# A fused two-block transformer kernel: new durations in the planner that orders its instructions

## The chip, the cores and the metric

One core of one Trainium2 chip runs the whole program. The metric is the device time of one execution in microseconds (us), the median of several runs; lower is better.

## What is computed

The input is 512 tokens of width 1024, all in fp32. The first block normalises x, projects it, runs three branches, merges them through sigmoid gates, and ends with a wide feed-forward layer. The second block has two layers, each of attention (eight softmax heads with a forget gate, eight retention heads), a gated convolutional feed-forward layer, and a gated addition. Cut to what matters here:

```python
h = rmsnorm(x, norm_mix_g)
a_q, a_k, a_v, b_q, b_f, b_i, b_g, c_q, c_kv, c_kr, gate_logits = split(h @ w_in)
y_a = chunked_relpos_attention(a_q, a_k, a_v, rel_bias)
y_b = hgrn2_recurrence(b_q, b_f, b_i, b_g, lower_bound, hgrn_norm_g)
y_c = mla_attention(c_q, c_kv, c_kr, positions, ...)
merged = sum(sigmoid(gate_logits[n]) * (y_n @ w_branch[n]) for n in branches)
x = x + merged @ w_out
x = x + square(relu(rmsnorm(x) @ w_ff1)) @ w_ff2
x = rmsnorm(x, final_norm_g)
for i in range(2):
    x = x + concat(forgetting_attention(...), retention(...)) @ w_out_2[i]
    x = x + (gelu(conv(up_a)) * up_g) @ w_down[i]
    x = x + sigmoid(rmsnorm(x) @ w_ple_gate[i]) * (p[i] @ w_ple_proj[i])
return rmsnorm(x, final_norm_w)
```

## The kernel before, in words

Activations lie feature-major: a tile of 128 features by 512 tokens. A projection (`proj`, `multi`, `group`; tiles `lin`) makes one block of 128 outputs. To keep fp32 precision, weights and activations are split into a high and a low half (`wh`, `wl`, `xh`, `xl`), and each 128-row step takes three passes on TensorE: `wh` with `xh`, `wl` with `xh`, `wh` with `xl` (`lin`, matmul line L379). A chunk of weights arrives by DMA as `raw`; ScalarE makes `wh` from it, VectorE makes `wl` (128x1024), and a finished block is taken out of PSUM by VectorE (`gate<-lin`, `qk<-lin`). The token-major values (`v`) are built in the same way.

Attention works by head: scores in `sc`, softmax on VectorE, ScalarE and GpSimd, transposes in `pt` (L389), the product with the values in `po`. The second branch (HGRN, functions `hgrn`, `hlev`, `level`, `dsplit`, `rsplit`) takes four pairs of heads. For each pair it walks nine levels of distance s = 1, 2, 4 ... 256. Per level ScalarE makes two exponentials (`eq`, `ek`), VectorE multiplies `eq` and updates two running sums (`suf`, `pre`), GpSimd multiplies `ek`, TensorE multiplies the two (`sc<-eq,ek`, with 64 contraction rows), and VectorE keeps the result (`dg`). After the last level VectorE makes the low halves (`sl`), TensorE takes the product with the values (`po<-sh,vs` and `po<-sl,vs`), and a per-head norm follows: ScalarE `tl`, VectorE `y`, ScalarE `sq`, TensorE transposes `gs`, VectorE `rs` and `ms`, GpSimd `rt` and `ex`, TensorE transposes `pb`, VectorE `qk`, ScalarE `xh`, VectorE `xl`. That `xh` and `xl` is the branch's output of the pair, `yb[pair]`. The merge of the branch (`up`) takes all four pairs: its first block can run nine passes on the first three pairs and then needs the fourth.

The order of the work is made while the program is built. Each piece of work is a coroutine (a Python generator); it writes out instructions and yields where the next one would have to wait. The projections form one long list of tasks (`stream`) at the lowest priority, and the driver (`drive`) takes them whenever no other coroutine is ready. "Ready" is judged by a clock kept in the program: `self.now` moves on by a number for each matmul (`mm`, `tr`), and for VectorE, ScalarE and GpSimd the class `Eng` adds up an estimated duration for each instruction (`net.busy`). A coroutine that waits for VectorE is taken up again when `self.now` has passed that engine's estimated end plus 200 ns (`w`, `LAT`). So these numbers choose how many passes of projections are put between two steps of a branch. Once built, every engine runs its own list strictly in the order written; semaphores alone hold it back. In the program all VectorE, ScalarE and GpSimd instructions are recorded through one line, L221.

## Time and profile before

| what | value |
|---|---|
| median of 3 runs | 2363.28 us (2362.02 to 2363.62) |
| profiled execution, span from first to last instruction | 2362.3 us |
| what lies around the span in the profiled execution | not shown; the median of the runs is 1.0 us above the span |
| TensorE busy | 2326.2 us, 98% of the span |
| VectorE busy | 1509.7 us, 64% |
| ScalarE busy | 1070.2 us, 45% |
| GpSimd busy | 455.0 us, 19% |
| mean granted TensorE clock | 0.994 |
| chain that ended last | 91% TensorE, 6% VectorE |

How to read it: TensorE is busy nearly the whole time, so the time is the passes plus the moments in which TensorE waits. Shares over the whole span say little about a stretch, and the stretch decides here: from 307 to 508 us the HGRN branch runs, with projections between its levels. The ends of matmuls are modelled, and the steps from start to start tell more than their durations.

### The profile page before, as it was taken

To read this page: it belongs to the slowest core of one execution; us is meant where nothing else is said; L and a number is where in the kernel's file an instruction comes from. 1 tells how busy PE (TensorE), PEld (TensorE's weight loads), DVE (VectorE), ACT (ScalarE), POOL (GpSimd) and SP (SyncE) were. 2 spreads that over 40 slices of the span, in tenths; PEclk is the share of its full clock that TensorE was granted. 3 is DMA by queue.
4 is the path that set the end of the run, shared out by engine and by line. 5 is a ranking of instruction groups with operands and counts; after the bars stand their busy time and mean duration, and the time that the engine had idled before them with its cause. 6 is when DMAs were issued, how large, how long until landed. Compare 5 with 4: busy or idle time off the path is not lost.

```text
span 2362.3 us, 28970 instructions
## 1 busy us (share of the span) xinstructions
PE 2326.2 (98%) x10810; PEld 1871.6 (79%) x10810; DVE 1509.7 (64%) x2355; ACT 1070.2 (45%) x1695; POOL 455.0 (19%) x531
## 2 busy tenths in 40 slices
PE   9999999999999999999999999999999999999998
PEld 7787877778888888777778888888777778888887
DVE  6778489976542554678866562457578866552466
ACT  5657466664321233555543331245555544331343
POOL 3423044431000002323330000002323320000012
PEclk9999999999999999999999999999999999999999
DMA  5222222223322332432332333333332332333332
GB/s 181 75 68 63 81 72 63 63 85 116 98 95 98 98 98 83 152 95 89 117 98 94 98 98 98 104 93 115 123 104 81 107 107 90 98 98 98 107 91 70
DMA packets 75725, 228.23 MB, mean 97 GB/s; under 512 B 9664, under 2 KB 15680, under 8 KB 75584
## 3 DMA queue, kind: packets, MB, share of 16 engines
q1 hardware_dynamic: 70400, 209.62, 28.2%
q0 software_dynamic: 5184, 16.75, 2.3%
q8 instruction: 85, 1.39, 0.3%
q14 instruction: 56, 0.46, 0.1%
HBM read 215.29 MB, written 6.32 MB: 94 GB/s over the span
## 4 chain that ended last, share of the span: by engine, by line
PE 91%; DVE 6%; issue 1%; ACT 1%; POOL 1%; DMA 0%; SPq 0%; POOLq 0%; DVEq 0%; ACTq 0%
PE lin L379 75%; PE v L379 6%; PE sc L379 5%; PE po L379 3%; PE pt L389 1%; DVE wl L221 1%; DVE dg L221 1%; DVE xl L221 1%; DVE eq L221 1%; DVE pre L221 0%; DVE suf L221 0%; DVE sl L221 0%; DVE gate L221 0%; ACT L221 0%; PE pb L389 0%
## 5 line engine op out<-in xcount | busy, mean ns | idle before, releaser
L379 PE MATMUL lin<-xh,wh 128*128 128x512 f32 (+1 forms) x2752 | 1095.9, 398 | 0.0
L379 PE MATMUL lin<-xl,wh 128*128 128x512 f32 (+1 forms) x2752 | 1072.4, 390 | 6.7 <-DVE xl L221 6.6
L379 PE MATMUL lin<-xh,wl 128*128 128x512 f32 (+1 forms) x2728 | 1061.8, 389 | 0.0
L221 DVE TENSOR_TENSOR wl<-raw,wh 128x1024 fp32r<-128x1024 f32 (+3 forms) x391 | 467.6, 1196 | 513.4 <-PE lin L379 335.7
L221 ACT ACTIVATE wh<-raw 128x1024 fp32r<-128x1024 f32 (+4 forms) x394 | 392.5, 996 | 821.7 <-PE lin L379 684.9
L379 PEld LDWEIGHTS lin<-xl,wh 128*128 128x128 f32 x2752 | 517.3, 188 | 117.7 <-DVE xl L221 8.8
L379 PEld LDWEIGHTS lin<-xh,wh 128*128 128x128 f32 x2752 | 517.4, 188 | 117.0 <-issue 11.7
L379 PEld LDWEIGHTS lin<-xh,wl 128*128 128x128 f32 x2728 | 514.2, 188 | 96.1
L221 POOL TENSOR_TENSOR sq<-sq 128x512 f32<-128x512 f32 (+1 forms) x61 | 90.6, 1485 | 571.5 <-ACT sq L221 570.8
L221 POOL TENSOR_SCALAR P<-P,r 128x128 f32<-128x128 f32 (+3 forms) x128 | 80.3, 633 | 198.7 <-DVE r L221 180.8
L221 POOL MEMSET pad<- 128x2 f32 x44 | 4.4, 100 | 586.7 <-DVE cv L221 586.7
L221 DVE SCALAR_TENSOR_TENSOR cv<-pad,vec,cv 128x512 f32<-128x512 f32 x88 | 66.1, 752 | 40.7 <-ACT cv L221 39.0
L221 DVE CUSTOM_DVE_ANT_0 lg<-sc,E 128x128 f32<-128x128 f32 (+1 forms) x96 | 46.6, 486 | 60.9 <-PE sc L379 53.7
L379 PE MATMUL v<-wh,xh 128*128 128x512 f32 x192 | 78.2, 407 | 2.3 <-POOL wh L221 2.3
L379 PE MATMUL v<-wl,xh 128*128 128x512 f32 x192 | 75.6, 394 | 1.5 <-DVE wl L221 1.4
L221 ACT ACTIVATE ph<-pt 128x512 fp32r<-128x512 f32 (+3 forms) x128 | 55.7, 435 | 45.5 <-PE pt L389 44.5
L379 PE MATMUL v<-wh,xl 128*128 128x512 f32 x192 | 75.5, 393 | 0.0
L221 ACT ACTIVATE P<-lg,m 128x128 f32<-128x128 f32 (+1 forms) x96 | 53.5, 558 | 39.7 <-DVE m L221 28.9
L221 DVE TENSOR_TENSOR x<-lin,x 128x512 f32<-128x512 f32 x80 | 54.6, 684 | 23.5 <-PE lin L379 23.4
L221 DVE TENSOR_TENSOR pl<-pt,ph 128x512 fp32r<-128x512 f32 (+3 forms) x128 | 60.4, 481 | 13.8 <-ACT ph L221 13.3
L221 ACT ACT_TABLE_LOAD x51 | 65.4, 1283 | 4.3 <-DVE qk L221 1.6
L221 ACT ACTIVATE tl<-po 64x512 f32<-64x512 f32 x56 | 33.2, 593 | 74.0 <-PE po L379 73.6
(243 smaller groups left out, 2558.6 us busy)
## 6 DMA issues: line engine op xcount, KB each, us to landing
raw<-wup SPq DMA_DIRECT2D x88, 512.0 KB, 3.3
raw<-w SPq DMA_DIRECT2D x83, 512.0 KB, 3.6
raw<-wf SPq DMA_DIRECT2D x64, 512.0 KB, 3.3
raw<-wdn SPq DMA_DIRECT2D x32, 512.0 KB, 3.5
raw<-wv SPq DMA_DIRECT2D x22, 512.0 KB, 3.6
raw<-wpg SPq DMA_DIRECT2D x16, 512.0 KB, 3.3
raw<-wbr SPq DMA_DIRECT2D x12, 512.0 KB, 3.3
raw<-wdn SPq DMA_DIRECT2D x16, 384.0 KB, 3.1
```

The source lines that it names most:

```text
L221: r = f(*a, **k)
L379: self.nc.tensor.matmul(out, l, r, start=start, stop=stop)
L389: self.nc.tensor.transpose(out, src, self.ident)
```

## The change

It replaces the numbers of the program's clock; nothing that is computed changes. A pass with 512 columns counts 226.8 ns where it counted 215.8; a switch between matmuls of 128 and of 64 contraction rows now counts 110 or 185 ns; VectorE counts 155 + 1.05 n ns where it counted 75 + 1.042 n + 60 per scalar operand; ScalarE 140 + 0.84 n + 60 per operand in place of 100 + 0.84 n + 93. GpSimd's numbers stay. Comments and docstrings are taken out too, which shifts line numbers (the matmul is L380, the transpose L394).

```diff
             if name == "dv":
-                d = 75.0 + 1.042 * n + 60.0 * ops
+                d = 155.0 + 1.05 * n
             elif name == "ac":
-                d = 100.0 + 0.84 * n + 93.0 * (ops + ("accum_out" in k))
+                d = 140.0 + 0.84 * n + 60.0 * (ops + ("accum_out" in k))
...
     def mm(self, out, l, r, start, stop):
         self.nc.tensor.matmul(out, l, r, start=start, stop=stop)
         n = int(np.prod(out.shape[1:]))
+        rows = 64 if l.shape[0] <= 64 else 128
+        if rows != self.rows:
+            self.now += 110.0 if rows == 64 else 185.0
+            self.rows = rows
         if l.dtype == F32:
-            self.now += 112.0 if n == 64 else max(218.0, n * 4 / 2.4 + 5)
+            self.now += 112.0 if n == 64 else 152.0 if rows == 64 else max(218.0, n * 4 / 2.4 + 27)
         elif l.dtype == BF16:
             self.now += n / 2.4 + 2.5
         else:
-            self.now += max(107.0, n / 2.4 + 2.5)
+            self.now += max(109.0, n / 2.4 + 13.5)
 
     def tr(self, out, src):
         self.nc.tensor.transpose(out, src, self.ident)
-        self.now += 112.0
+        self.rows = 128
+        self.now += 109.0
```

The change moves instructions on all engines, by the thousand, since every later choice follows from an earlier one. Two places matter most; both lie at the end of the HGRN branch, at its fourth pair.

TensorE, last product with the values of the fourth pair, before:

```order
L379 MATMUL po<-sh,vs 128x128
L379 MATMUL po<-sl,vs 128x128
L379 MATMUL lin<-xh,wh 128x512
L379 MATMUL lin<-xh,wl 128x512
L379 MATMUL lin<-xl,wh 128x512
```

and now:

```order
L380 MATMUL po<-sh,vs 128x128
L380 MATMUL po<-sl,vs 128x128
L394 MATMUL gs<-cst,sq 128x128 x4
L394 MATMUL pb<-cst,ex 128x128 x4
L380 MATMUL lin<-xh,wh 128x512
L380 MATMUL lin<-xh,wl 128x512
L380 MATMUL lin<-xl,wh 128x512
```

Before, 21 projection passes stand between the product and the transposes `gs`, and 27 more between `gs` and `pb`. Now none stand there; `pb` follows `gs` at once, and the next passes are those that need the fourth pair's output.

VectorE, the norm of the same pair, before:

```order
L221 TENSOR_TENSOR y<-po,tl 64x512 x2
L221 TENSOR_TENSOR wl<-raw,wh 128x1024
L221 TENSOR_TENSOR gate<-lin,rb 128x512
L221 TENSOR_REDUCE rs<-gs 128x8
L221 TENSOR_SCALAR ms<-rs 128x8
```

and now:

```order
L221 TENSOR_TENSOR y<-po,tl 64x512 x2
L221 TENSOR_REDUCE rs<-gs 128x8
L221 TENSOR_SCALAR ms<-rs 128x8
L221 SCALAR_TENSOR_TENSOR qk<-y,vec,qk 128x512
L221 TENSOR_TENSOR qk<-pb,qk 128x512
L221 TENSOR_TENSOR xl<-qk,xh 128x512
```

The weight halves (`wl`) and the gates' blocks (`gate<-lin`) that stood between the steps of the norm are done earlier now, among the levels of the pairs.

## Rows read from the trace of the kernel before

**Rows 1.** The page, part 1: the span, and TensorE's busy time.

```profile
span 2362.3 us, 28970 instructions
PE 2326.2 (98%) x10810; PEld 1871.6 (79%) x10810; DVE 1509.7 (64%) x2355; ACT 1070.2 (45%) x1695; POOL 455.0 (19%) x531
```

**Rows 2.** Waits of TensorE: line waited for what, us in total, times, longest.

```profile
PE lin L379 <- DVE xl L221: 6.6, 4, 2.4
PE sc L379 <- DVE eq L221: 5.8, 10, 1.1
```

**Rows 3.** Stretches: length, busy PE, PEld, DVE, ACT, POOL, granted clock, DMA.

```profile
307.00:358.00 51.00, 47.27 (x282) 36.61 (x281) 47.33 (x75) 34.47 (x49) 21.57 (x17) 1.00 0.23 67
358.00:408.00 50.00, 46.76 (x285) 36.14 (x283) 47.88 (x75) 31.27 (x47) 22.92 (x18) 1.00 0.20 61
408.00:458.00 50.00, 45.45 (x275) 35.84 (x275) 46.85 (x74) 32.09 (x46) 24.05 (x19) 0.97 0.19 63
458.00:508.00 50.00, 48.60 (x293) 38.64 (x291) 45.99 (x72) 37.06 (x50) 18.26 (x15) 1.00 0.24 72
508.00:534.00 26.00, 25.98 (x126) 21.03 (x125) 13.13 (x19) 11.91 (x17) 5.21 (x6) 1.00 0.30 97
```

**Rows 4.** The chain that ended last, first feed-forward layer: start, length, what.

```profile
607.16 342.76 PE lin L379 x1512
```

**Rows 5.** Groups of VectorE from 306 to 534 us: busy us, mean ns.

```profile
L221 DVE TENSOR_TENSOR wl<-raw,wh 128x1024 fp32r<-128x1024 f32 x29 | 39.3, 1356 | 7.0 <-PE lin L379 5.5 <-issue 1.2 <-ACT ek L221 0.3
L221 DVE TENSOR_TENSOR gate<-lin,rb 128x512 f32<-128x512 f32 x16 | 10.9, 683 | 2.8 <-PE lin L379 2.7
```

**Rows 6.** Timeline of the fourth pair's end: start us, length us, engine and operation.

```profile
508.54 1.14 PE L379 MATMUL sc<-eq,ek 64*128 64x256 f32 x8
...
515.90 0.59 ACT L221 ACTIVATE tl<-po 64x512 f32<-64x512 f32 x1 [1.60 <-PE po L379]
...
516.52 0.69 DVE L221 TENSOR_TENSOR y<-po,tl 64x512 f32<-64x512 f32 x1 [1.96 <-ACT tl L221]
...
517.25 0.63 ACT L221 ACTIVATE sq<-y 128x512 f32<-128x512 f32 x1
...
521.13 0.69 DVE L221 TENSOR_REDUCE rs<-gs 128x8 f32<-128x512 f32 x1
...
522.11 1.65 POOL L221 TENSOR_TENSOR rt<-ms,cst 128x8 f32<-128x8 f32 x1 [3.59 <-DVE ms L221]
523.84 0.62 POOL L221 TENSOR_SCALAR ex<-rt 128x512 f32<-128x512 f32 x1
...
527.08 0.60 PE L389 MATMUL pb<-cst,ex 128*128 128x128 f32 x4
527.71 0.69 DVE L221 TENSOR_TENSOR qk<-pb,qk 128x512 f32<-128x512 f32 x1 [0.16 <-PE pb L389]
528.44 0.63 ACT L221 ACTIVATE xh<-qk 128x512 fp32r<-128x512 f32 x1 [0.88 <-DVE qk L221]
...
532.88 0.68 DVE L221 TENSOR_TENSOR xl<-qk,xh 128x512 fp32r<-128x512 f32 x1
```

**Rows 7.** Timeline: TensorE after a wait at a feed-forward layer's start.

```profile
1239.84 0.79 PE L379 MATMUL lin<-xl,wh 128*128 128x512 f32 x1 [2.43 <-DVE xl L221]
1240.43 0.63 PE L379 MATMUL lin<-xh,wh 128*128 128x512 f32 x1
1240.85 0.63 PE L379 MATMUL lin<-xh,wl 128*128 128x512 f32 x1
```

**Rows 8.** Timeline: projection passes behind a level's scores.

```profile
451.41 0.50 PE L379 MATMUL lin<-xh,wh 128*128 128x512 f32 x1
...
451.75 0.39 PE L379 MATMUL lin<-xh,wl 128*128 128x512 f32 x1
```

**Rows 9.** Timeline: one `wl` beside a product on GpSimd.

```profile
497.70 1.30 POOL L221 TENSOR_TENSOR ek<-k,ek 128x512 f32<-128x512 f32 x1 [6.32 <-PE lin L379]
...
497.76 2.32 DVE L221 TENSOR_TENSOR wl<-raw,wh 128x1024 fp32r<-128x1024 f32 x1
```

More of the change, by code (lines that the diff above doesn't have):

```diff
@@ L385, in mm @@
         else:
-            self.now += max(107.0, n / 2.4 + 2.5)
+            self.now += max(109.0, n / 2.4 + 13.5)
     def tr(self, out, src):
         self.nc.tensor.transpose(out, src, self.ident)
-        self.now += 112.0
+        self.rows = 128
+        self.now += 109.0
     def consts(self):
```

## The prediction

> **What bounds the kernel now.** I read the page's first part, then TensorE's waits, then the busy times by stretch, and last the timeline of the places that those named. The first part gives the frame: TensorE is busy 2326.2 of 2362.3 us [rows 1]. The change adds and removes no pass; both programs hold the same 10546 matmuls of the same shapes, and both switch between 128 and 64 contraction rows 384 times. So order alone can act, and only on the some 36 us in which TensorE does not work, on the clock it is granted, and on the small cost of going from one kind of matmul to another.
>
> The waits name two owners inside the span: projection passes that wait for `xl` from VectorE, 6.6 us, and HGRN scores that wait for `eq` from VectorE, 5.8 us in ten places [rows 2]. The first is at the start of the two gated feed-forward layers. There the new order has the same VectorE list (`x`, `xl`, `wl`, `x`, `xl` ...) as the old one, so I cost it at no change. The second belongs to the HGRN branch, and the stretches show what the waits alone hide. From 307 to 508 us TensorE is busy 47.27 + 46.76 + 45.45 + 48.60 = 188.1 of 201 us, and VectorE 47.33 + 47.88 + 46.85 + 45.99 = 188.05 of 201, 93.6% [rows 3]. Both are nearly full, but VectorE can not be helped by order: its list has no slack to give. From 508 to 534 us VectorE is half idle and TensorE full, 25.98 of 26 [rows 3]: there projections cover the norm of the fourth pair.
>
> **The change, term by term.** Everything is counted against the profiled execution with its 2362.3 us; the median of the runs is 1.0 us above that span.
>
> *The HGRN levels.* In the old order 591 projection passes stand between the branch's first scores and the last level's scores of the fourth pair; in the new one 678. A pass takes 342.76 / 1512 = 0.2267 us [rows 4], so 87 passes, or 19.7 us of cover, move in front of that point. TensorE had 201 - 188.1 = 12.9 us idle there, and half clock cost 3% of one stretch of 50 us, 1.5 us [rows 3]; together 14.4 us that the moved passes can fill. The last scores began at 508.5 us [rows 6]. TensorE alone could reach them at 508.5 + 19.7 - 14.4 = 513.8 us. VectorE is later: with the 87 passes, four more `wl` (24 before, 28 now) and four more gate blocks (20, then 24) come ahead of that point, 4 x (1.356 + 0.683) = 8.2 us [rows 5]. 188.05 + 8.2 = 196.2 us of work at the same 93.6% takes 209.7 us in place of 201, so the last scores begin 8.7 us later, at 517.2 us. I take this value, since VectorE was the fuller of the two in three of the four stretches.
>
> *The fourth pair's end.* Before, 87 passes filled this chain: 9 and 6 around the first product with the values, the 21 and the 27 of the order shown, and 24 behind `pb`. Now nothing does. From the scores: 1.14 us of scores; some 0.8 us until the first `sl` is there (a ScalarE and a VectorE step like `sq` and `y`, 0.63 + 0.69, less half of the scores); both products with the values, 5120 columns or ten passes, 2.3 us; `tl`, `y`, `sq` from 515.90 to 517.88, 1.98 us; `gs`, taken like `pb`, 0.60; `rs` to the end of `ex`, 521.13 to 524.46, 3.33 us; `pb` 0.60; `qk` and `xh` from 527.71 to 529.07 and `xl` 0.68 behind it, 2.1 us [rows 6]. With some 0.15 us of handing over that is 13.0 us, of which TensorE idles 8.2. So `xl` is ready at 517.2 + 13.0 = 530.2 us; before it was at 532.88 + 0.68 = 533.56 us [rows 6], with TensorE hardly waiting. That is a gain of 3.4 us.
>
> *The clock after these gaps.* Behind the wait of 2.43 us the steps from start to start are 0.42 us [rows 7], the half clock of 1.2 GHz, where a pass else takes 0.2267. Seven or eight passes at +0.2 us cost 1.6 us. The new chain has gaps of 0.8, 2.0, 3.3 and 2.1 us with little work between. The least is nothing, the most four times 1.6; I take one and a half times, 2.4 us, since the gaps lie so near each other that one slow stretch may span two. The Trainium skill (TensorE: Matmul & The Clock Gate, Part 1: The HAM clock gate) says that the array falls back to half its clock when it idles, and that gaps that come back pay it each time; by that the term would be the full four times, 6.4 us. No row here shows four gaps in a row. The branch as a whole then stands at -3.4 + 2.4 = -1.0 us.
>
> *Returns to projections.* A projection pass behind other work costs more: its step is 451.75 - 451.41 = 0.34 us [rows 8] and not 0.227, 0.11 us more. Counted in the order, a run of projections is broken 341 times before, 324 now. Five of the 17 fewer lie in the HGRN branch, where TensorE is not the bound, four more come in the first attention stretch, and sixteen fewer in the two layers: twelve that count, 1.3 us saved. The two bounds are none and 17 x 0.11 = 1.9 us.
>
> *Attention in the two layers.* The new order puts, in the first layer, a weight half `wl` ahead of a low half `pl` of the probabilities at two heads, and the product with the values right behind. Nothing in the trace of before shows that wait. A `wl` takes 1.36 us on the mean [rows 5], so two of them bound the loss at 2.7 us; below, it is nothing, since other passes may be long enough. I take 0.5 us, near the lower end, because among the longest waits of TensorE none is for `pl` [rows 2].
>
> ScalarE loads a table of functions 57 times and not 51; ScalarE has room in the HGRN stretches (34.47 of 51 us busy, 31.27 to 37.06 of 50 [rows 3]), and I cost it at nothing; if that cover were gone it would lengthen the levels, which belongs to the rival below.
>
> The sum: -1.0 - 1.3 + 0.5 = -1.8 us on 2362.3, or 2360.5 us of span, and 1.0 us more for a median: **2361.5 us**.
>
> **The rivals.** *VectorE fills its gaps (faster).* Its fullest stretch shows 47.88 of 50 us, 95.8% [rows 3]. If the better spaced order keeps it at that, 196.2 us of work take 204.9 us and TensorE's own 513.8 us becomes the bound: 3.4 us earlier, and with one slow stretch of the clock 0.8 us less. The time is 2361.5 - 4.2 = 2357.3 us. For it: that share was reached over one stretch of 50 us, in the old order. Against it: the new numbers still leave something out. A `wl` counts 155 + 1.05 x 1024 = 1230 ns, and it took 1356 on the mean [rows 5] and 2.32 us where it began 0.06 us behind a product on GpSimd [rows 9]. The Trainium skill (SBUF — State Buffer, SBUF: two separate sides) states that a VectorE operation with two SBUF inputs and a GpSimd one lock each other out of one pair of ports; the row fits that, and it speaks against a plan with one number per size.
>
> *VectorE starves behind later scores (slower).* `dg` stands in VectorE's list right behind the scores it copies, and all that follows waits with it. The new order puts up to 30 passes between two levels where 12 to 24 stood. By the end of the second pair it has 60 more passes in front, 13.6 us, while TensorE's idle time up to there was 3.73 + 3.24 = 7.0 us [rows 3], and VectorE's extra work there is three `wl`, 4.1 us. So the scores would come 13.6 - 7.0 - 4.1 = 2.5 us behind VectorE, which idles for that long. If that happens at each of the four pairs, 10 us are lost, and the time is 2371.5 us. It decides from the point at which VectorE's share from 307 us to the last scores falls under 91%: 196.2 us of work in 216 us or more. Against it: by the end of the third pair 66 passes, 15.0 us, stand against 3.73 + 3.24 + 4.55 us of idle time and 1.5 us of half clock, 13.0 us, so the two about balance there.
>
> *Every gap pays the clock (a rule above).* Four slow stretches, 6.4 us in place of 2.4: 2365.5 us, still within what the measurement can tell from no change.
>
> *The change does less than it says.* Outside attention the order is nearly the same: 1512 and twice 1590 projection passes in one run stand unbroken in both programs. If all that moved lies under cover, the time is 2363 us; this is the forecast's neighbour and has no price of its own.
>
> **How the numbers follow.** A measurement of this kernel tells 0.2%, 4.7 us, from no change. The forecast with its neighbour has 0.46, the clock 0.12, the fast rival 0.24, the slow one 0.18. Forecast and clock are both within 0.2%: same 0.58. The fast rival's 2357.3 is 6.0 us below the median: faster 0.24. The slow one: slower 0.18. The range goes from the fast rival with all 1.9 us of returns and no wait in the layers, 2357.3 - 0.6 - 0.5, and another 1 us for a VectorE without waits, 2355, up to nearly the slow rival's 2371.5, to 2370.
>
> **What would show it.** Right: in the stretch from 307 us to the last scores of the fourth pair VectorE is again busy 93 to 95%, the waits for `eq` shrink to under 3 us, and the last scores come near 517 us; behind them four waits of TensorE, of 0.8 to 3.4 us, for `sl`, `sq`, `ex` and `xl`; the granted clock shows half for one or two short stretches there. The waits for `xl` at the feed-forward layers stay near 6.6 us. Wrong: the last scores at 514 us or earlier (the fast rival), or at 522 us or later with VectorE under 91% (the slow one), or new waits of TensorE in the two layers of over 3 us together.

## The result, and the profile after

The change is slower: 2375.99 us, median of 4 runs (2373.89 to 2378.30), against 2363.45 us (2362.02 to 2365.72) for the kernel before beside it; the ratio is 1.0052, 95% interval 1.0038 to 1.0066. The profiled execution took 2374.39 us, with a span of 2372.6 us. The loss is 12.5 us; the forecast was 2361.5.

The first part of the change's page stands beside [rows 1]. TensorE is busy 3.3 us more and the span is 10.3 us longer, so most of the loss is time in which TensorE does nothing:

```profile
span 2372.6 us, 28991 instructions
PE 2329.5 (98%) x10810; PEld 1876.6 (79%) x10810; DVE 1509.1 (64%) x2355; ACT 1077.2 (45%) x1701; POOL 462.1 (19%) x531
```

TensorE's waits over the whole span (line, waited for what, us in total, times, longest), beside [rows 2]:

```profile
PE sc L380 <- DVE eq L221: 8.5, 8, 1.7
PE lin L380 <- DVE xl L221: 6.7, 4, 2.4
PE pb L394 <- POOL ex L221: 4.3, 2, 3.8
PE sc L380 <- POOL ek L221: 2.9, 1, 2.9
...
PE gs L394 <- ACT sq L221: 2.1, 1, 2.1
PE lin L380 <- ACT xh L221: 1.5, 1, 1.5
```

Two lines of the kernel before belong beside these, and [rows 2] does not show them:

```profile
PE sc L379 <- POOL ek L221: 3.0, 1, 3.0
...
PE pb L389 <- POOL ex L221: 0.4, 1, 0.4
```

The waits for `xl` at the feed-forward layers are what they were (6.6, now 6.7), and so is the one for GpSimd's `ek` (3.0, now 2.9). The waits for `eq` did not shrink, they grew from 5.8 to 8.5, those for `ex` grew from 0.4 to 4.3, and `sq` and `xh` are new.

Where does the time go? I set the n-th projection pass of the one trace beside the n-th of the other. Up to the last pass that can do without the fourth pair's output the change is ahead, 14.1 us at the most and 8.8 us at the last. Over the next 14 passes it falls back by 18.7 us, to 9.9 us behind. From there to the last pass, through the feed-forward stages and both layers, the distance comes back to between 9.8 and 10.1 us after every detour in the layers' attention: 9.9 at the end. So the loss shows at the end of the HGRN branch. The timeline of TensorE there (start us, length us, and in brackets the idle time ahead of it and what ended it), beside [rows 6]:

```profile
525.66 1.14 PE L380 MATMUL sc<-eq,ek 64*128 64x256 f32 x8 [1.34 <-DVE eq L221]
527.44 0.50 PE L380 MATMUL po<-sh,vs 128*128 128x512 f32 x1 [0.64 <-ACT sh L221]
...
532.83 1.12 PE L394 MATMUL gs<-cst,sq 128*128 128x128 f32 x4 [2.13 <-ACT sq L221]
537.80 1.11 PE L394 MATMUL pb<-cst,ex 128*128 128x128 f32 x4 [3.85 <-POOL ex L221]
540.42 0.80 PE L380 MATMUL lin<-xh,wh 128*128 128x512 f32 x1 [1.50 <-ACT xh L221]
541.01 0.63 PE L380 MATMUL lin<-xh,wl 128*128 128x512 f32 x1
541.44 0.63 PE L380 MATMUL lin<-xl,wh 128*128 128x512 f32 x1
```

The last scores begin at 525.66 us (before: 508.54). Behind them stand four waits and then 13 passes at steps of 0.43 us, the half clock.

Two stretches sort this out, here first of the change and then of the kernel before: from the branch's first scores to the fourth pair's last, and from there past the branch's end. The columns are those of [rows 3]; length less PE busy is TensorE's idle time.

```profile
304.50:525.70 221.20, 207.59 (x1225) 164.69 (x1223) 199.54 (x300) 152.08 (x207) 91.50 (x67) 0.99 0.22 67
525.70:561.70 36.00, 27.65 (x114) 21.89 (x115) 21.53 (x33) 11.33 (x17) 5.61 (x6) 0.81 0.25 81
```

```profile
306.10:508.50 202.40, 189.48 (x1136) 148.23 (x1134) 189.31 (x293) 136.28 (x192) 86.80 (x67) 0.99 0.22 66
508.50:551.70 43.20, 43.18 (x202) 35.46 (x202) 28.25 (x39) 18.39 (x26) 5.21 (x6) 1.00 0.32 104
```

At the levels TensorE idled 12.9 us before and 13.6 us now, though 87 more passes stand among them: they took nothing off. Behind the last scores it idled 0.0 us before and 8.4 us now. With half clock (1.7 and 0.2 us before, 1.7 and 2.8 now, summed from the steps) that is 26.5 - 14.8 = 11.7 us, nearly the whole loss. The branch's first scores begin 1.6 us earlier in the change (304.5 against 306.1), which leaves 10.1 of the 10.3 us by which its span is longer.

### The profile page after: what moved, and what is told of

Its sections match the earlier page's. It is cut to its first block, busy times and chain, and to the rows that moved or that the text cites. A ratio compares the mean times of both kernels' runs of the same rounds, so it can differ in the third digit from the quotient of the medians.

```text
span 2372.6 us, 28991 instructions
## 1 busy us (share of the span) xinstructions
PE 2329.5 (98%) x10810; PEld 1876.6 (79%) x10810; DVE 1509.1 (64%) x2355; ACT 1077.2 (45%) x1701; POOL 462.1 (19%) x531
## 4 chain that ended last, share of the span: by engine, by line
PE 93%; DVE 4%; issue 1%; POOL 1%; ACT 0%; DMA 0%; SPq 0%; POOLq 0%; DVEq 0%; ACTq 0%
PE lin L380 76%; PE sc L380 6%; PE v L380 6%; PE po L380 3%; PE pt L394 1%; DVE wl L221 1%; DVE xl L221 1%; DVE eq L221 0%; DVE pre L221 0%; PE pb L394 0%; DVE dg L221 0%; POOL f L221 0%; DVE suf L221 0%; PE bc L394 0%; PE cs L394 0%
## 5 line engine op out<-in xcount | busy, mean ns | idle before, releaser
L380 PE MATMUL lin<-xh,wh 128*128 128x512 f32 (+1 forms) x2752 | 1094.8, 398 | 1.5 <-ACT xh L221 1.5
L380 PE MATMUL lin<-xl,wh 128*128 128x512 f32 (+1 forms) x2752 | 1073.1, 390 | 6.7 <-DVE xl L221 6.7
L380 PE MATMUL lin<-xh,wl 128*128 128x512 f32 (+1 forms) x2728 | 1062.6, 390 | 0.0
L380 PEld LDWEIGHTS lin<-xh,wh 128*128 128x128 f32 x2752 | 518.3, 188 | 119.0 <-issue 11.3
L380 PEld LDWEIGHTS lin<-xl,wh 128*128 128x128 f32 x2752 | 518.1, 188 | 117.6 <-DVE xl L221 8.6
L380 PEld LDWEIGHTS lin<-xh,wl 128*128 128x128 f32 x2728 | 515.1, 189 | 96.9
L380 PE MATMUL v<-wh,xh 128*128 128x512 f32 x192 | 78.5, 409 | 0.8 <-POOL wh L221 0.8
L380 PE MATMUL v<-wl,xh 128*128 128x512 f32 x192 | 75.8, 395 | 1.3 <-DVE wl L221 1.3
L380 PE MATMUL v<-wh,xl 128*128 128x512 f32 x192 | 75.6, 394 | 0.0
L221 DVE TENSOR_TENSOR pl<-pt,ph 128x512 fp32r<-128x512 f32 (+3 forms) x128 | 60.5, 482 | 10.3 <-ACT ph L221 10.0
L221 POOL TENSOR_TENSOR ek<-k,ek 128x512 f32<-128x512 f32 x32 | 50.7, 1586 | 75.2 <-ACT ek L221 68.3
```

The lines of the kernel that those rows point to most:

```text
L221: r = f(*a, **k)
L380: self.nc.tensor.matmul(out, l, r, start=start, stop=stop)
```

## The experiments

Three questions: is it the end that has lost its cover; which number of the change does it; and why did 87 passes among the levels take nothing off the waits there?

**One account for all.** "Levels" is TensorE's idle time from the branch's first scores to the fourth pair's last, "behind" the idle time after that up to the end of the branch, both by stretches as above; "half" is what the passes at half clock cost in both, by their steps. "Ahead" is the number of projection passes ahead of the last scores. All other columns are in us. The sums come from one profiled execution of each kernel, the medians from 4 to 10 executions.

| run | ahead | levels | behind | half | sum | median |
|---|---|---|---|---|---|---|
| before | 591 | 12.9 | 0.0 | 1.9 | 14.8 | 2363.4 |
| the change | 678 | 13.6 | 8.4 | 4.5 | 26.5 | 2376.0 |
| VectorE's numbers only | 666 | 7.8 | 7.4 | 3.5 | 18.7 | 2367.6 |
| all but VectorE's | 567 | 16.9 | 0.0 | 2.5 | 19.4 | 2368.5 |
| three gates held back | 597 | 21.8 | 0.0 | 4.7 | 26.5 | 2375.3 |
| latency -200 ns | 606 | 18.5 | 0.0 | 1.7 | 20.2 | 2378.5 |
| short GpSimd product | 678 | 1.4 | 8.4 | 2.8 | 12.6 | 2361.3 |
| planner knows contention | 675 | 14.1 | 9.1 | 2.6 | 25.8 | 2378.2 |
| same, latency -100 ns | 594 | 13.5 | 0.0 | 2.6 | 16.1 | 2367.1 |
| before, planner knows it | 591 | 16.1 | 0.0 | 2.1 | 18.2 | 2368.0 |
| before, ln k | 507 | 10.8 | 0.0 | 2.4 | 13.2 | 2363.7 |
| change, ln k, latency -100 | 585 | 5.9 | 0.0 | 1.6 | 7.5 | 2359.5 |

The median less the sum lies between 2348 and 2353 in all rows but one (latency -200 ns, which also changes the layers). So this one stretch of the program decides, and the runs of the table can be read by their sums to within some 5 us. The other eight runs are read by their own rows below.

### Which number does it

Kernel before, VectorE's durations alone:

```diff
-                d = 75.0 + 1.042 * n + 60.0 * ops
+                d = 155.0 + 1.05 * n
```

> Only VectorE's durations are replaced; TensorE's, the row modes' and ScalarE's stay as before. In its order 666 projection passes stand ahead of the fourth pair's last scores (591 before, 678 in the change), and none between its last product with the values and its norm. Theory 'uncovered end' (the loss is the fourth pair's closing chain, which has no passes left beside it): as slow as the change, 2372 to 2378 us. Rival 'TensorE's numbers' (the dearer passes and row modes pull the work forward): 2361 to 2366 us.

Measured: 2367.55 us (2366.22 to 2368.81), ratio 1.0015 (1.0006 to 1.0025). The change with that line undone:

> All of the change but VectorE's durations. 567 passes stand ahead of the fourth pair's last scores, 111 are left for its closing chain. 'Uncovered end': 2359 to 2366 us. Rival 'TensorE's numbers': 2371 to 2378 us. Rival 'starved VectorE' (the loss arises at the levels, wherever scores stand behind more passes): between the two, 2364 to 2371 us.

Measured: 2368.53 us, ratio 1.0021 (1.0011 to 1.0031). Neither part does it alone: the first run lies between the ranges of its two theories, the second in that of 'starved VectorE'. The stretches of the first, then of the second:

```profile
306.50:518.70 212.20, 204.43 (x1213) 162.39 (x1211) 196.61 (x299) 152.70 (x207) 86.39 (x67) 0.99 0.22 70
518.70:555.30 36.60, 29.18 (x126) 23.51 (x126) 22.75 (x33) 12.64 (x18) 5.61 (x6) 0.86 0.24 79
```

```profile
304.40:506.70 202.30, 185.39 (x1114) 145.93 (x1112) 186.35 (x289) 134.26 (x190) 87.24 (x68) 0.98 0.20 62
506.70:555.60 48.90, 48.90 (x228) 40.55 (x228) 30.21 (x41) 19.67 (x27) 5.21 (x6) 1.00 0.33 107
```

VectorE's longer durations pull the passes forward and uncover the end (7.4 us behind), but the levels gain 5.1 us by it. The other numbers (dearer passes, row modes, ScalarE's durations) do the reverse: the end stays covered, the levels wait 4.0 us more. Together they have the bad side of both.

### Is it the uncovered end

Three gates' blocks held back in the change until the last scores are written:

```diff
         for m in range(KT):
+            if m == KT - 3:
+                self.tasks.append(self.hold)
             self.gate(1, m, N, gs[m])
...
+    def hold(self):
+        yield lambda: self.bend
```

> The change, with the last three gates' blocks (72 passes) held back until the fourth pair's last scores are written. All that lies ahead of them keeps the change's order; the last levels of the fourth pair have fewer passes between them, its closing chain has 81 again. 'Uncovered end': 2360 to 2367 us, since the 18.7 us lost at the branch's end go and only the last levels' waits grow. 'Starved VectorE': 2373 to 2378 us, the levels' order before is untouched. Rival 'give and take' (what the end gains the last levels lose): 2372 to 2376 us.

Measured: 2375.33 us (2370.72 to 2377.39). The end is covered, and nothing is won: the fourth pair's last levels, with hardly a pass between them, wait instead (stretches, then the longest of the waits from 500 to 525 us).

```profile
304.70:518.10 213.40, 191.63 (x1142) 152.43 (x1141) 191.50 (x289) 139.66 (x194) 89.77 (x67) 0.96 0.20 62
518.10:562.90 44.80, 44.79 (x194) 36.31 (x195) 29.35 (x44) 18.50 (x26) 6.15 (x6) 0.93 0.31 100
```

```profile
PE sc L380 <- DVE eq L221: 8.9, 4, 2.8
```

So my first theory, that covering the end again would be enough, falls. The rival in that expectation (give and take) holds.

More passes beside the end, without touching the levels. The merge's first six blocks take their first three steps ahead of the fourth pair's output, in one task:

```diff
+            for m in range(mm):
+                ps = yield from self.psr("lin", max(mm, self.lincap), "lin")
+                yield from self.lin(ps, w[m // 2], 512 * (m % 2), ys[:-1], True, False)
+                pss.append(ps)
+            for m in range(mm):
+                yield from self.lin(pss[m], w[m // 2], 512 * (m % 2) + 384, ys[-1:], False, True)
+                self.spawn(evac(m)(pss[m]), 0)
```

> The change, with the merge's first six blocks taken up to their third step before the fourth pair's output is needed: 45 more passes (10.2 us at 0.2267 us) can run beside the closing chain; the levels are not touched, apart from passes that come where the stream had run dry. 'Uncovered end': 9 to 11 us faster than the change, 2364 to 2368 us. 'Starved VectorE' or a loss in the layers: within 2 us of the change, 2374 to 2378 us.

Measured: 2371.22 us (2369.09 to 2376.87). Then staged: the last three blocks only once `gs` is written, and the next low half of the weights earlier:

```diff
+                if m == 3:
+                    yield lambda: self.gsn >= 4
```

> The change with the merge's first six blocks taken to their third step ahead of the fourth pair's output, as in the run before, but the last three of them only once gs is written, and the next weights' low half made two blocks earlier. 696 passes stand ahead of gs (723 there), 717 ahead of pb. 'Late branch' with an uncovered end: gs and pb come some 4 us earlier than there, the waits for ex (4.1 us) and for wl (3.1 us) go, 2362 to 2367 us. Rival (what is won comes back as another wait in the merge): 2369 to 2373 us.

Measured: 2370.79 us (2368.63 to 2373.24). The same on VectorE's durations alone:

> Only VectorE's durations are replaced, and the merge is staged as in the run above: 666 passes ahead of the fourth pair's last scores, 696 ahead of gs, 720 ahead of pb. With VectorE's durations alone TensorE waits least at the levels, and 10.8 us were lost in waits and half clock at the end (2.4 us for sq, 4.1 for ex, 1.9 for xh, 2.4 of half clock). 'Late branch' with an uncovered end: most of that goes, 2357 to 2361 us, faster than both kernels. Rival (the closing chain gets later by the passes put ahead of it): 2364 to 2369 us.

Measured: 2365.55 us, ratio 1.0008 (0.9999 to 1.0017). And once more with every second block's sum on GpSimd:

```diff
-                    eng = self.dv if last else self.pl
+                    eng = self.dv if last and (m + j) % 2 == 0 else self.pl
```

> Only VectorE's durations replaced, the merge staged, and every second block's sum in the last merge made by GpSimd in place of VectorE. In the staged run TensorE waited 1.3, 2.7 and 1.4 us for the merged blocks' low halves, which VectorE makes behind a product and a sum for each block. If VectorE's queue in the merge was the new wait: the 5.4 us fall to under 3, 2361 to 2363.5 us, faster than before or the same. If not: 2365 to 2367 us.

Measured: 2366.41 us, ratio 1.0008 (0.9999 to 1.0017). Ten us of passes beside the end (an estimate: 45 passes at 0.2267 us) give some 5 us back in the change and 2 us with VectorE's durations alone. All four runs miss the range of their first theory; the three staged ones lie in those of their rivals. TensorE's waits from 520 to 570 us in the staged change show what took the rest:

```profile
PE lin L380 <- DVE xl L221: 3.9, 3, 2.3
PE gs L394 <- ACT sq L221: 2.1, 1, 2.1
```

The merge is now pressed into a shorter time, and the low halves of its blocks, which VectorE makes, come late. GpSimd's sums did not mend that (4.8 us in three waits for `xl` there, 4.0 without them).

The closing chain made shorter by its norm, in the change and in the kernel before:

```diff
-        pb = yield from self.gnorm(yv, EPS)
+        if pr < 3:
+            pb = yield from self.gnorm(yv, EPS)
```

> The change without the fourth pair's per-head norm: sq, gs, rs, ms, rt, ex, pb and the product with pb are left out, so that pair's output is not normalised; the order of all else stays. In the change TensorE waited 2.3 us for sq, 4.2 for ex and 1.9 for xh there, then ran 13 passes at half clock (2.8 us). 'Uncovered end': the waits for sq and ex go with 0.9 us of transposes, perhaps the half clock too, 2366 to 2369 us. If the closing chain's length does not decide (TensorE would wait as long for something else): 2373 to 2377 us.

> The kernel before with the same left out (the fourth pair's per-head norm). There 87 passes lie beside the closing chain. 'Uncovered end' of the change alone: the norm is hidden here, its transposes' 0.9 us and no more are saved, 2361.5 to 2364 us. If the norm were exposed in both: 2354 to 2358 us.

Measured: 2373.11 us (2370.53 to 2374.16) and 2361.28 us (2360.29 to 2362.78), 2.9 us under the change, and 2.7 us under the kernel before as it ran beside this one (ratio 0.9990, 0.9981 to 1.0000). The first missed the 2366 to 2369 us of 'uncovered end' and lies in the rival's range, so by medians the norm counts about as much in either kernel. The traces tell more: in the change the idle time behind the scores falls from 8.4 to 5.1 us, and in the kernel before it was nothing and stays so. Half of the chain remains (product, `tl`, `y`, `qk`, `xh`), and the wait for `xh` grows from 1.5 to 4.2 us.

The clock by itself: 49 matmuls of constants in the waits of the closing chain.

```diff
+        for _ in range(n):
+            self.nc.tensor.matmul(t[:, 0:384], self.idb, self.mkb, start=True, stop=True)
```

> The change with 49 matmuls of bf16 constants (128x384) on TensorE in the waits of the fourth pair's closing chain: 14 ahead of gs, 24 ahead of pb, 11 behind it. They read constants, wait for nothing and nobody reads them. If the half clock behind those waits is a separate cost, it goes: the 13 passes that took 0.2 us more each are at full speed, 2373.2 us (2372 to 2374.5), with a granted clock of 1.0 there. If the clock falls all the same, or the dummies push gs or pb later by what they save: 2375 to 2379 us.

Measured: 2374.03 us (2370.56 to 2376.54), 2.0 us under the change and within the expected range; but the spreads of the two overlap, so the gain in time is not shown. The granted clock is. First the change, from ahead of `gs` to the 13th pass; then this run, ahead of the first constants and from them on:

```profile
532.70:546.30 13.60, 8.12 (x22) 6.02 (x23) 4.28 (x7) 1.34 (x3) 5.03 (x6) 0.50 0.20 58
```

```profile
530.80:534.10 3.30, 3.30 (x14) 3.11 (x13) 0.79 (x2) 0.59 (x1) 0.00 (x0) 0.50 0.00 0
534.20:562.10 27.90, 27.90 (x142) 20.86 (x141) 19.08 (x28) 9.46 (x13) 5.62 (x6) 1.00 0.25 85
```

In the change TensorE runs at half clock from just ahead of `gs` on: through both transposes, the waits for `ex` and `xh`, and the 13 passes. With the constants all of that is at full clock. A shorter stretch at half clock lies ahead of the first constants, on the product with the values, which takes 4.8 us there and 3.3 in the change.

### Why the levels gave nothing back

Fewer passes at each step, by a shorter latency in the planner:

```diff
-    LAT=200.0,
+    LAT=-200.0,
```

> The change with the planner's latency at -200 ns in place of 200: every wait of a coroutine is planned 400 ns shorter, so fewer projection passes come between any two steps. 606 passes stand ahead of the fourth pair's last scores (591 before, 678 in the change), and 615, 633 and 654 ahead of its product, gs and pb. Theory 'late branch' (more passes are put between the levels than TensorE waits there, so each pair ends later, and at the fourth nothing is left beside its closing chain): the branch ends as before, 2360 to 2367 us, with the fourth pair's gs within 3 us of where it stands before. Rival 'levels' (with shorter blocks TensorE waits more at the levels, as in the run with all but VectorE's durations): 2367 to 2373 us. Rival 'it lies elsewhere, in what the dearer passes and row modes do to the order': 2373 to 2378 us.

Measured: 2378.47 us (2377.45 to 2380.23). The number is just above the third theory's range, but the trace shows the second: 18.5 us of idle time at the levels, and the branch ends 7.7 us behind the kernel before. The other 7.3 us come later, in the layers and the closing norm, which plan with the same latency.

Less work for VectorE, order kept:

```diff
+            if n == 1:
+                self.nc.scalar.activation(out.h, ps, AF.Copy)
+                self.busy["dv"] = max(self.busy["dv"], self.now) + 155.0 + 1.05 * S
```

> The change with the eight gates' blocks of the HGRN branch taken out of PSUM by ScalarE (a copy; the multiplication by 1/rms is left out) in place of VectorE; the planner still counts VectorE's duration, so the order of every engine stays. 8 x 0.683 = 5.5 us of VectorE's work go from the stretch of the third and fourth pair's levels. 'VectorE bounds the levels' (step (a) of the forecast): the fourth pair's last scores come 4 to 5.5 us earlier, 2370 to 2372 us. 'VectorE starves' (it waits for scores that stand behind passes, so its load is not what counts): last scores within 1.5 us of the change's, 2374.5 to 2377.5 us.

Measured: 2377.57 us (2373.14 to 2379.07). VectorE is busy 4.1 us less in the stretch, and TensorE idles 13.3 us there in place of 13.6:

```profile
305.00:525.90 220.90, 207.64 (x1223) 164.65 (x1222) 195.40 (x292) 155.19 (x214) 91.91 (x67) 0.99 0.21 68
```

So a lighter load for VectorE does not shorten the levels' waits (ScalarE is busy 3.1 us more by the edit, which this run does not separate). The timeline ahead of one of the change's three longest waits at a level (VectorE, GpSimd, and TensorE's weights and scores at its end) shows what they wait for:

```profile
319.90 0.41 DVE L221 TENSOR_TENSOR suf<-suf,pre 128x256 f32<-128x256 f32 x1
320.06 1.41 POOL L221 TENSOR_TENSOR gate<-gate 128x512 f32<-128x512 f32 x1 [3.62 <-DVE gate L221]
320.35 1.40 DVE L221 TENSOR_TENSOR pre<-pre 128x256 f32<-128x256 f32 x1
321.44 3.12 POOL L221 TENSOR_TENSOR ek<-k,ek 128x512 f32<-128x512 f32 x2
321.68 1.75 DVE L221 TENSOR_TENSOR eq<-qk,eq 128x512 f32<-128x512 f32 x1
...
323.55 0.33 PEld L380 LDWEIGHTS sc<-eq,ek 64*128 64x128 f32 x4 [2.05 <-POOL ek L221]
323.58 0.38 PE L380 MATMUL sc<-eq,ek 64*128 64x128 f32 x2 [1.65 <-DVE eq L221]
```

The weights waited for `ek` and the scores for `eq`; `eq` ended last, at 323.43 us. `suf` and `pre` are steps of the same size. Ahead of GpSimd's `gate` such a step takes 0.41 us, beside it 1.40; `eq`, 0.68 us elsewhere, takes 1.75 beside `ek`. The new numbers of the planner are those of undisturbed steps (155 + 1.05 x 256 = 424 ns, 155 + 1.05 x 512 = 693 ns). So I cut GpSimd's product short, order kept:

```diff
-            self.pl.tensor_tensor(out=ek, in0=k, in1=ek, op=ALU.mult)
+            self.nc.gpsimd.tensor_tensor(out=ek[:, 0:8], in0=k[:, 0:8], in1=ek[:, 0:8], op=ALU.mult)
+            self.busy["gp"] = max(self.busy["gp"], self.now) + 75.0 + 2.3 * S
```

> The change with GpSimd's product for ek cut from 512 columns to 8 (the rest of ek stays without the factor k); the planner still counts the full one, so the order of every engine stays. In the change's trace a VectorE instruction that reads two operands from SBUF takes about 1 us more where it meets a GpSimd product (eq 1.75 us in place of 0.68, pre 1.40 in place of 0.41), and such a step stands ahead of most of the levels' longer waits. Theory 'GpSimd beside VectorE makes the levels late, and the planner does not know it': the levels' waits shrink by 8 us or more, 2362 to 2369 us. Rival 'the waits come from passes being dealt in blocks': within 3 us of the change, 2373 to 2377 us.

Measured: 2361.29 us (2355.44 to 2363.15), 14.7 us under the change, a little more than expected. The order is the change's, and the idle time at the levels falls from 13.6 to 1.4 us; what lies behind the scores is the same to a tenth.

```profile
304.20:510.80 206.60, 205.18 (x1223) 163.32 (x1222) 184.15 (x300) 150.60 (x206) 52.19 (x67) 1.00 0.23 72
510.80:546.90 36.10, 27.71 (x114) 21.96 (x115) 21.57 (x33) 12.08 (x18) 5.63 (x6) 0.81 0.25 80
```

The groups of VectorE and GpSimd from 303 to 526 us (count, busy us, mean ns of one), first of the change, then of this run:

```profile
L221 DVE TENSOR_TENSOR eq<-qk,eq 128x512 f32<-128x512 f32 x36 | 27.8, 772 | 0.0
L221 DVE TENSOR_TENSOR suf<-suf,pre 128x256 f32<-128x256 f32 x32 | 18.4, 576 | 0.3 <-ACT ek L221 0.3
L221 POOL TENSOR_TENSOR ek<-k,ek 128x512 f32<-128x512 f32 x32 | 50.7, 1586 | 75.2 <-ACT ek L221 68.3 <-issue 2.6 <-DVE dg L221 2.1
```

```profile
L221 DVE TENSOR_TENSOR eq<-qk,eq 128x512 f32<-128x512 f32 x36 | 24.6, 684 | 0.0
L221 DVE TENSOR_TENSOR suf<-suf,pre 128x256 f32<-128x256 f32 x32 | 13.8, 431 | 0.3 <-ACT ek L221 0.3
L1383 POOL TENSOR_TENSOR ek<-k,ek 128x8 f32<-128x8 f32 x32 | 13.2, 414 | 90.0 <-ACT ek L221 80.5 <-issue 3.6 <-PE lin L380 3.0
```

That the levels wait because of GpSimd's product is shown. VectorE is busy 15.4 us less in this stretch with the same 300 instructions (199.54, now 184.15). How much of the gain is VectorE's steps beside the product, and how much the product's own length on the way to the scores, is not shown: this run takes both away together. TensorE's waits in the change name `eq` for 8.5 us and `ek` for 2.9.

Can the planner be told? In these runs, inside the branch, a VectorE step of two SBUF operands waits in the plan until a GpSimd product that it meets is over:

```diff
+                a, b = net.gpi
+                if a < t0 + d and t0 < b:
+                    d += b - max(a, t0)
```

The second of the three also has, as the last run below, a shorter latency inside the branch:

```diff
-        return max(0.0, max(self.busy[e] for e in engs) - self.now) + self.LAT
+        return max(0.0, max(self.busy[e] for e in engs) - self.now) + (-100.0 if self.lk else self.LAT)
```

> The change, and inside the HGRN branch the planner also lets a VectorE instruction with two SBUF operands wait until a GpSimd product ends that it meets. 675 passes stand ahead of the fourth pair's last scores (678 in the change) and none beside its closing chain, as in the change; the blocks between the levels are of other sizes. Theory 'unknown contention': the levels wait less, 5 us or more come off, 2366 to 2371 us, and the 12 us lost at the end stay. Rival 'any placement with this many passes ahead costs the same': 2373 to 2378 us.

> As the run with the planner that knows the contention, and inside the branch its latency is -100 ns in place of 200, so fewer passes are taken at each step: 594 stand ahead of the fourth pair's last scores, 603, 618 and 639 ahead of its product, gs and pb (591, 600, 627, 654 before). Nothing outside the branch is planned otherwise than in the change. Theory 'unknown contention' with an end that is covered again: as good as before or better, 2357 to 2364 us. Rival 'levels' (fewer passes, longer waits there, as with the latency of -200 everywhere): 2367 to 2372 us.

> The kernel before with the planner that knows the contention inside the branch. 591, 600, 627 and 654 passes stand ahead of the fourth pair's last scores, product, gs and pb, exactly as before; only the blocks ahead of them are of other sizes. Theory 'unknown contention': the levels wait 3 us or more less, 2358 to 2361 us, faster than before. Rival: 2362 to 2366 us.

Measured: 2378.23 us (2374.86 to 2382.62), 2367.10 us (2365.69 to 2369.14) and 2368.02 us (2366.88 to 2370.25). None reaches what its theory asked for, and none is faster than the kernel before. The second is 8.9 us faster than the change, with an end that is covered again. For the first, the stretches to 458 us and from there to the last scores tell why, here of the change and then with the planner that knows:

```profile
307.00:458.00 151.00, 140.97 (x848) 111.54 (x846) 140.51 (x210) 95.94 (x134) 66.99 (x49) 1.00 0.23 69
458.00:525.70 67.70, 64.12 (x364) 51.02 (x364) 56.63 (x87) 53.67 (x72) 24.51 (x19) 0.97 0.20 64
```

```profile
307.00:458.00 151.00, 145.02 (x863) 115.46 (x864) 139.67 (x205) 102.17 (x138) 66.23 (x51) 1.00 0.22 69
458.00:525.10 67.10, 58.98 (x356) 46.82 (x352) 59.49 (x92) 49.95 (x69) 21.65 (x17) 0.97 0.22 71
```

Up to 458 us the better plan does fill: 6.0 us idle in place of 10.0, with 486 passes from the first scores on in place of 468. That leaves 189 for the rest in place of 210, and the rest idles 8.1 us in place of 3.6. A fixed stock of passes was moved, and the waits moved the other way. The third run idles 16.1 us at the levels, the kernel before 12.9, with the same 591 passes ahead; these runs do not show why.

So the next two runs take the product itself away. ScalarE takes ln k once for each pair, and the running sum starts from it; then `exp(suf)` is `ek`, and 32 GpSimd products fall away:

```diff
-        self.pl.memset(suf, 0.0)
...
+        self.ac.activation(suf, k, AF.Ln)
...
-        if ek is not k:
-            self.pl.tensor_tensor(out=ek, in0=k, in1=ek, op=ALU.mult)
```

> The kernel before without GpSimd's product k x exp(suf): ScalarE takes ln k once per pair, the running sum suf starts from it in place of 0, and exp(suf) is ek at once. 32 GpSimd products leave the levels; nothing else is computed otherwise. The planner, with the numbers of before, puts 507 passes ahead of the fourth pair's last scores and leaves 171 beside its closing chain. Theory 'GpSimd beside VectorE makes the levels late': the run with the short GpSimd product took 14.5 us of the levels' waits away; here the end is covered too, so it is faster than both kernels, 2349 to 2358 us. Rival 'what the levels gain, the smaller blocks give back': 2360 to 2365 us.

> The same edit on the change, with the planner's latency inside the HGRN branch at -100 ns, so that the end keeps its cover: 585 passes ahead of the fourth pair's last scores, 597, 615 and 636 ahead of its product, gs and pb. Theory: the levels wait 10 us or more less than in the change and the 12 us lost at its end do not come, 2349 to 2357 us. If the new numbers only pay with a covered end, it is faster than the same edit on the kernel before by 1 us or more. Rival: as slow as the run with the contention told to the planner and the same latency, 2364 to 2369 us.

Measured on the kernel before: 2363.68 us (2361.28 to 2365.93), ratio 0.9999 (0.9990 to 1.0008). Its planner now thinks the levels ready earlier and takes 84 passes fewer ahead of the last scores, so what the levels gain is given back, as the rival had it. On the change with the shorter latency in the branch: 2359.50 us (2356.11 to 2362.74), ratio 0.9983 (0.9973 to 0.9992), faster than both kernels. The stretches of this one:

```profile
302.60:498.40 195.80, 189.86 (x1129) 149.88 (x1129) 174.47 (x292) 137.01 (x194) 41.93 (x32) 0.97 0.21 65
498.40:544.60 46.20, 46.20 (x216) 38.33 (x216) 30.86 (x41) 18.79 (x26) 5.21 (x6) 1.00 0.33 109
```

5.9 us idle at the levels, none behind. It missed its expectation of 2349 to 2357 by 2.5 us.

## Why the prediction was wrong, point by point

**The HGRN levels: the step that failed.** The forecast let the 87 moved passes fill TensorE's idle time and half clock, so that the last scores came at 513.8 us by TensorE and at 517.2 by VectorE. They came at 525.7. Idle time went from 12.9 to 13.6 us, half clock stayed at 1.7: of the 14.4 us that the passes were to fill they filled nothing, and the stretch from the first to the last scores grew by 221.2 - 202.4 = 18.8 of their 19.7 us. The amount of VectorE's work was right (196.2 us forecast, 197.04 measured up to there). That it stays 93.6% busy was not:

```profile
307.00:525.60 218.60, 205.04 (x1210) 162.48 (x1208) 197.04 (x296) 149.51 (x205) 91.50 (x67) 0.99 0.22 67
```

90.1%. The step that failed took idle time for room in which any pass fits. The runs show that it is waits of single levels that hang on GpSimd's product: with the product cut short, in the same order, the last scores come at 510.8 us, even ahead of the 513.8 that the forecast gave TensorE alone (the first scores begin 1.9 us earlier there than before), and 1.4 us of idle time are left. That the 87 passes stood at other levels than these waits is the likely reason why they shortened nothing; it was not tested by itself.

Two signs were in hand. [rows 9] shows a VectorE step stretched beside a GpSimd product; it stood as an argument against the fast rival, and no term had its price. And the forecast named two owners of TensorE's waits, where the list of the kernel before has GpSimd's `ek` third, with 3.0 us. The run with the short product gives the price of the product: 14.7 us of time. It also shows that a full VectorE was partly a VectorE beside GpSimd: 15.4 of its 199.5 us at the levels go with the product.

**The fourth pair's end: mechanism right, size near.** 13.0 us were forecast from the last scores to `xl`. In the change `xl` is made at 540.39 in 0.69 us, so it is ready at 541.08, 15.4 us behind the scores; 1.0 us of the difference are the two transposes at half clock (1.12 and 1.11 us, where `pb` took 0.60 before). TensorE was to idle 8.2 us and idled 8.4; its last wait was for `xh`, not for `xl`. But the chain starts 8.5 us later than forecast, so the expected gain of 3.4 us there became a loss of 541.08 - 533.56 = 7.5 us.

**The clock.** 2.4 us were forecast and 2.8 measured, in 13 passes behind the chain; that the two are so near is in part luck. The granted clock fell once, just ahead of `gs`, after waits of 0.64 and 0.22 us and at the end of one of 2.13, and stayed at 1.2 GHz up to the 13th pass. The waits for `ex` and `xh` lay inside this stretch, and the transposes' 1.0 us, which it cost too, stood in no term. The rival in which each gap pays (6.4 us) did not come. The rule of the Trainium skill that it drew on (TensorE: Matmul & The Clock Gate, Part 1: The HAM clock gate), that gaps that come back pay each time, is not what this trace shows: here four gaps cost one slow stretch between them.

**Returns to projections and the layers' attention.** The forecast was -1.3 and +0.5 us. From the end of the branch to the last pass the distance of the two traces changes by 0.1 us, so neither term shows in the layers. The feed-forward layers' waits stayed, as said.

**The rivals.** VectorE starving behind later scores is what the marks say: last scores at 522 us or later (525.7), VectorE under 91% (90.1%). It was given 18%, and its 2371.5 us is 4.5 us short of the median; 2.4 us of that is that the profiled span lies 3.4 us under the median here and 1.0 before. Its reason is another matter. VectorE's wait for scores, up to the last scores, before, in the change and with the short product:

```profile
DVE dg L221 <- PE sc L379: 9.4, 13, 1.3
DVE dg L221 <- PE sc L380: 11.4, 10, 2.2
DVE dg L221 <- PE sc L380: 13.2, 10, 2.4
```

VectorE does wait longer for scores in the change, as this rival says. But it waits longest with the short product, where TensorE idles only 1.4 us at the levels. So this wait is not what costs the time; the reason the runs show is GpSimd's product. The fast rival, with VectorE filling its gaps, failed on the same point as the forecast.

**Still open.** Why VectorE's numbers alone leave 7.8 us at the levels and all numbers together 13.6, with nearly as many passes ahead, was not taken apart further; nor was why telling the planner of the contention makes the kernel before slower. The two log runs differ in latency and numbers at once, so the change's numbers are not shown to be the better ones.

## What to carry to other kernels

A planner deals out a fixed stock of cover. A number that takes more of it early has to be paid where the stock ends, so count what is left beside the last chain before counting what is filled; and idle time counts as room only at the very waits where the new passes stand. Durations taken from a trace as one number per size leave out what engines do to each other; here the only kernel that computes everything and was faster than the one before took away the instruction that disturbs and shortened the planner's latency in the branch; taking the instruction away alone changed nothing (2363.68 us).

## What the runs showed of the hardware

VectorE steps with two SBUF operands took about 1 us more when a GpSimd product ran beside them (0.41 to 1.40, 0.68 to 1.75 us), while steps that read PSUM did not (`gate<-lin` keeps a mean of 681 ns in the change). The Trainium skill (SBUF — State Buffer, SBUF: two separate sides) states that such a VectorE operation and one on GpSimd that reads SBUF hold one pair of ports by turns, each for its whole instruction; the rows fit that. What was not expected is what this does to a third engine: with the product cut short, TensorE idles 12.2 us less at the levels, though that counts the product's own length too.

In the closing chain of the change four waits of TensorE lay within 15 us; the granted clock fell once, at the end of the second, and 13 passes behind the last still ran at half clock. With 49 matmuls of bf16 constants laid into the chain from behind the product to ahead of these passes, the granted clock was 1.00 from the first constant on.
